# Two of eight hidden chunks of an MLP's second product as seven block products instead of eight

## The chip, the cores and the metric

One core of one Trainium2 chip runs the whole program. The metric is the device time of one execution in microseconds. The engines are named as the profile names them: PE is TensorE (PEld its weight loads), DVE is VectorE, ACT is ScalarE, SP is the engine that issues the loads.

## The reference

A decoder trunk of two layers on 512 tokens of width 1024, float32. Each layer has a mixer (not touched here), a layer norm, and an MLP with a residual and a second layer norm:

```python
def sqrelu_mlp(x, w1, w2):
    return jnp.square(jax.nn.relu(x @ w1)) @ w2
...
x = layer_norm(ALPHA * x + sqrelu_mlp(x, w_ff1[layer], w_ff2[layer]), ln2_g[layer], ln2_b[layer])
```

`w_ff1` is 1024x4096 and `w_ff2` 4096x1024, for each of the two layers.

## The kernel before

**Arithmetic.** Each float32 operand is split in two float32r parts, a rounded one ("hi", a cast on ScalarE) and the rest ("lo", a subtraction on VectorE). A product is then three matmuls: hi by hi, hi by lo, lo by hi.

**First product.** The hidden width is done in eight groups. Group g covers 256 columns of each half of `w_ff1`, and the activations are halved by rows and by columns, so a group is a 2x2 block matrix times a 2x2 block matrix. Group 0 is done with the eight plain block products. Groups 1 to 7 use the seven products of Strassen and Winograd, named P1, P2 and p3 to p7 (`PRODUCTS`). A product is 24 matmuls of 256 columns. The weight sums t1 to t4 are made on VectorE (line 374). The results are put together on VectorE (lines 485 to 498) from PSUM banks and two SBUF rows V and X. A bank may be shared: `RELEASED` says that p7 and p4 accumulate on one bank, "d", and P1 and P2 on another, "a". For block C22 the bank "d" is read when it holds p7 alone (line 485); for block C21 it is read when it holds p7 and p4 (line 493). V needs p6, X needs V and p5, and C22 needs X and p7.

**Activation.** `relu2` makes relu, square and the hi part of a hidden block on ScalarE (lines 428 to 430). The lo part (line 431, VectorE) is put on the list `late`, which is emitted at the next step by `flush`.

**Second product.** Chunk c of it uses the hidden blocks of group c. For each column half n and each token tile t it does twelve matmuls of 512 columns into one bank (`ff2_half`), and VectorE adds the bank to the residual XN (`add_half`, line 208). That is eight halves, 96 matmuls and eight additions for a chunk. Chunks 6 and 7 are done last, together with the layer norm.

**Order.** PE and VectorE keep the order of the program here; ScalarE's order is set by the framework's planner. The list `slots` is PE's order: group 1, chunk 1, group 2, chunk 2, groups 3 and 4, chunk 3, group 5, chunk 4, group 6, chunk 5, group 7, and the close. Inside a group the order (`LATER`) is P1, p5, p7, p6, p3, P2, p4. The list `wseq` is the order in which weight blocks are summed and split; `upto` issues loads up to six entries and splits up to six entries ahead of PE. At each slot the program emits, in this order, the weight work of `upto`, the lo parts of `flush`, the matmuls, and the VectorE work that reads their bank. Six PSUM banks rotate (`cycle`). Raw weight blocks (512 KB each) lie in three places of tag "raw" for `w_ff2` and in two of tag "cr" and two of tag "xk" for `w_ff1`. Eight pairs of split weights can be live.

Of the kernel before, what the change touches and what calls it, by code (L numbers as in the profile page):

```python
# [103 lines left out]
def trunk(ctx: ExitStack, tc: tile.TileContext, a: dict, out: bass.AP):  # L104
# [177 lines left out]
    ff_T = {}  # L282

    def ff(layer, hp, fp, xp, out_proj, prefetch):
# [66 lines left out]
        raws, got_w, kept2 = {}, {}, {}  # L351
        BLOCK = {"B11": (0, 0), "B12": (0, 1), "B22": (1, 1), "B21": (1, 0)}
        SUM = {"t1": ("B11", "B12"), "t3": ("B12", "B22"), "t2": ("t1", "B22"), "t4": ("t2", "B21")}

        def load1(g, n):

            for m in (n,) if g == 0 else {"B11": ("B11", "B12"), "B21": ("B21",), "t1": ("B22",)}.get(n, ()):
                if g == 0 and m != "B22":
                    raw = wp.tile([P, WG], F32, tag="raw", name="raw", bufs=3)
                elif g == 0 or m in ("B11", "B12"):  # L360
                    raw = xp.tile([P, WG], F32, tag="cr", name="cr", bufs=2)
                else:
                    if g not in kept2:
                        kept2[g] = xp.tile([P, 2, WG], F32, tag="xk", name="cr2")
                    raw = kept2[g][:, m == "B21"]
                raws[g, m] = raw
                nc.sync.dma_start(raw.rearrange("p (k c) -> p k c", k=HK_), w1v(*BLOCK[m], g))

# [17 lines left out]
        def terms1(g, n):  # L386
# [7 lines left out]
            else:  # L394
                hi, lo = pair(EARLY[n] if g == 0 else None)
                split(hi, lo, raw)
                his, los = ([z.rearrange("p (k c) -> p k c", k=HK_)[:, :, tb(j)] for j in range(2)] for z in (hi, lo))
            got_w[g, n] = his, los

        def load2(c, n, half):  # L400
            r = half * 2048 + c * GF
            raw = wp.tile([P, WG], F32, tag="raw", name="raw", bufs=3)
            nc.sync.dma_start(raw.rearrange("p (k c) -> p k c", k=2),
                              w2[r:r + GF, n * 512:(n + 1) * 512].rearrange("(k p) c -> p k c", p=P))
            raws["w2", c, n, half] = raw
# [29 lines left out]
        late = []  # L435

        def flush():
            while late:
                late.pop(0)()
# [23 lines left out]
        def product(g, n):  # L463
# [9 lines left out]
            V = LG[:, g % 2 * 512:(g % 2 + 1) * 512]  # L473
            X = LB[:, g % 2 * 512:(g % 2 + 1) * 512]
# [28 lines left out]

        def ff2_half(c, n, t):
# [9 lines left out]
        LATER = ("P1", "p5", "p7", "p6", "p3", "P2", "p4")  # L514
        slots, wseq = [], []

        def put_group(g):
            slots.extend((g, n) for n in LATER)
            wseq.extend((g, n) for n in ("B11", "t1", "t3", "t2", "B22", "B21", "t4"))

        def put_chunk(c):
            slots.extend(("w2", c, n, t) for n in range(2) for t in range(NT))
            wseq.extend(("w2", c, n, h) for n in range(2) for h in range(2))
# [3 lines left out]

        mid = NG // 2 - 1
# [824 lines left out]
```

## Time and profile before

| | us |
|---|---|
| median of three runs | 1167.61 (1167.41 to 1168.32) |
| the profiled execution | 1168.8 |
| its span, first to last instruction | 1167.1 |
| PE busy in the span | 1142.6 |
| VectorE busy in the span | 827.2 |

PE is busy for nearly the whole span, so the time is read stage by stage: what PE does there, and where it waits. A busy PE of the profile is modelled, so the pace of matmuls is taken from the length of a stretch and the number of its matmuls.

### The profile page before, as it was taken

The numbers are of one execution on the slowest core, as the hardware profiler recorded it, in microseconds if no ns is written. First come the engines' busy times: TensorE is split into PE (matmuls) and PEld (weight loads), VectorE is DVE, ScalarE is ACT, GpSimd is POOL, SyncE is SP. The second block draws the span as 40 slices with busy tenths as digits, with TensorE's granted clock in tenths as the row PEclk, the third lists the DMA queues.
The fourth block names the chain that finished last, engine by engine and source line by source line (L and its number), as shares of the span: only waits on it lengthen the run. The fifth ranks groups of instructions, "written<-read, shape, count | busy, mean of one in ns | idle before, by whom it ended". The sixth has DMA issues, their size and how long they took to land.

```text
span 1167.1 us, 17136 instructions
## 1 busy us (share of the span) xinstructions
PE 1142.6 (98%) x6888; PEld 996.6 (85%) x6888; DVE 827.2 (71%) x1562; ACT 516.1 (44%) x801; POOL 5.0 (0%) x13
## 2 busy tenths in 40 slices
PE   8999999999999999999999999999999999999997
PEld 8988788898889998998888888778997899889986
DVE  6745687786766767657758559898767577676655
ACT  5467462444343634533254433443544437345330
POOL 0000000000000000000000000000000000000000
PEclk9999999999999999999999999999999999999999
DMA  7413143133412342224235312212133224314121
GB/s 254 140 37 108 55 132 104 37 109 109 126 57 88 127 126 74 89 74 140 72 98 145 90 55 73 73 61 67 59 125 117 85 85 144 127 38 127 54 90 55
DMA packets 84207, 111.68 MB, mean 96 GB/s; under 512 B 6080, under 2 KB 53056, under 8 KB 84128
## 3 DMA queue, kind: packets, MB, share of 16 engines
q1 hardware_dynamic: 84128, 110.59, 30.1%
q8 instruction: 54, 0.88, 0.3%
q14 instruction: 25, 0.20, 0.1%
HBM read 108.47 MB, written 2.10 MB: 95 GB/s over the span
## 4 chain that ended last, share of the span: by engine, by line
PE 88%; DVE 7%; ACT 4%; DMA 0%; issue 0%; SPq 0%; DVEq 0%; ACTq 0%
PE f L451 23%; PE f L161 10%; PE f L159 10%; PE f L160 10%; PE vg L159 3%; PE vg L160 3%; PE vg L161 3%; PE op L159 2%; PE op L161 2%; PE op L160 2%; PE sc L836 1%; PE qk L159 1%; PE qk L160 1%; PE qk L161 1%; PE o L858 1%; PE pl L1117 1%
## 5 line engine op out<-in xcount | busy, mean ns | idle before, releaser
L161 PE MATMUL f<-whi,hl 128*128 128x512 f32 x448 | 178.0, 397 | 5.5 <-DVE hl L431 5.5
L159 PE MATMUL f<-whi,hh 128*128 128x512 f32 x448 | 177.9, 397 | 1.3 <-ACT hh L430 1.3
L164 ACT CAST whi<-cr 128x1024 fp32r<-128x1024 f32 x98 | 100.8, 1048 | 174.7 <-PE f L161 81.4
L160 PE MATMUL f<-wlo,hh 128*128 128x512 f32 x448 | 177.3, 396 | 0.0
L165 DVE TENSOR_TENSOR wlo<-cr,whi 128x1024 fp32r<-128x1024 f32 x98 | 119.2, 1220 | 23.0 <-ACT whi L164 23.0
L451 PE MATMUL f<-XH,wlo 128*128 128x256 f32 x448 | 125.9, 281 | 0.0
L451 PE MATMUL f<-XH,whi 128*128 128x256 f32 x448 | 125.8, 281 | 0.0
L451 PE MATMUL f<-XL,whi 128*128 128x256 f32 x448 | 125.8, 281 | 0.0
L161 PEld LDWEIGHTS f<-whi,hl 128*128 128x128 f32 x448 | 84.7, 189 | 27.8 <-DVE hl L431 8.1
L208 DVE SCALAR_TENSOR_TENSOR XN<-XN,f 128x512 f32<-128x512 f32 (+1 forms) x113 | 74.3, 678 | 43.9 <-PE f L161 43.1
L159 PEld LDWEIGHTS f<-whi,hh 128*128 128x128 f32 x448 | 84.7, 189 | 21.1 <-ACT hh L430 2.1
L160 PEld LDWEIGHTS f<-wlo,hh 128*128 128x128 f32 x448 | 84.8, 189 | 19.3
L451 PE MATMUL f<-sl,whi 128*128 128x256 f32 x336 | 94.5, 281 | 0.0
L451 PE MATMUL f<-sh,wlo 128*128 128x256 f32 x336 | 94.5, 281 | 0.0
L451 PE MATMUL f<-sh,whi 128*128 128x256 f32 x336 | 94.4, 281 | 0.0
L431 DVE TENSOR_TENSOR hl<-r,hh 128x512 fp32r<-128x512 f32 x64 | 44.1, 690 | 60.5 <-ACT hh L430 60.5
L451 PEld LDWEIGHTS f<-XL,whi 128*128 128x128 f32 x448 | 84.4, 188 | 0.5
L451 PEld LDWEIGHTS f<-XH,whi 128*128 128x128 f32 x448 | 84.4, 188 | 0.5
L451 PEld LDWEIGHTS f<-XH,wlo 128*128 128x128 f32 x448 | 84.4, 188 | 0.0
L164 ACT CAST whi<-raw 128x1024 fp32r<-128x1024 f32 x56 | 58.0, 1050 | 54.0 <-PE f L451 35.7
L137 ACT CAST whi<-raw 128x1024 fp32r<-128x1024 f32 (+3 forms) x61 | 60.2, 991 | 47.6 <-DMA raw<-in_w_in_odd 18.8
L138 DVE TENSOR_TENSOR wlo<-raw,whi 128x1024 fp32r<-128x1024 f32 (+3 forms) x61 | 69.7, 1148 | 14.6 <-ACT whi L137 14.3
(270 smaller groups left out, 2528.7 us busy)
## 6 DMA issues: line engine op xcount, KB each, us to landing
raw<-in_w_ff SPq DMA_DIRECT2D x70, 512.0 KB, 4.1
cr<-in_w_ff SPq DMA_DIRECT2D x58, 512.0 KB, 4.0
raw<-in_w_in_odd SPq DMA_DIRECT2D x24, 512.0 KB, 4.0
XN<-in_x SPq DMA_DIRECT2D x16, 256.0 KB, 3.0
raw<-in_w_in_even SPq DMA_DIRECT2D x8, 512.0 KB, 3.8
raw<-in_w_out_even SPq DMA_DIRECT2D x8, 512.0 KB, 3.6
raw<-in_w_out_odd SPq DMA_DIRECT2D x8, 512.0 KB, 3.5
LB<-in_ln_b SPq DMA_DIRECT2D x4, 512.0 KB, 3.8
```

Of the source, the lines that this page charges most:

```text
L137: nc.scalar.copy(hi[:, :n], raw[:, :n])
L138: nc.vector.tensor_tensor(lo[:, :n], raw[:, :n], hi[:, :n].bitcast(F32), ALU.subtract)
L159: nc.tensor.matmul(acc, lh, rh, start=first, stop=False)
L160: nc.tensor.matmul(acc, lh, rl, start=False, stop=False)
L161: nc.tensor.matmul(acc, ll, rh, start=False, stop=last)
L164: nc.scalar.copy(hi, src)
L165: nc.vector.tensor_tensor(lo, src, hi.bitcast(F32), ALU.subtract)
L208: nc.vector.scalar_tensor_tensor(x, x, ALPHA if first else 1.0, acc, ALU.mult, ALU.add)
L431: late.append(lambda: nc.vector.tensor_tensor(f(hl), r, f(hh).bitcast(F32), ALU.subtract))
L451: nc.tensor.matmul(d, l, r, start=first and j == k == i == 0, stop=j == 1 and k == HK_ - 1 and i == 2, skip_group_check=True)
L836: nc.tensor.matmul(sc[:, :N], qts[t][:B_QK, h, :], KT[:, h, :N], start=True, stop=True)
L858: nc.tensor.matmul(os[t][:, h, :], pT[:, j * P:(j + 1) * P], V[:, j, h, :], start=j == 0, stop=j == t)
```

## The change

Chunks 2 and 4 of each layer are now done as seven block products as well (`product2`), of twelve matmuls of 512 columns each, 84 for a chunk. For that the four hidden blocks of groups 2 and 4 are kept in float32 and four sums of them, s1 to s4, are made on VectorE and cast on ScalarE (`h_sum`); A21 alone needs no split. Four sums of the raw weight blocks of `w_ff2` are made on VectorE, and seven instead of four weight blocks are split. Each product leaves two banks. Those of P1 and p6 go to an SBUF row pair V2, those of the other five straight to XN; V2 is added to three blocks of XN after chunk 4. All raw weight blocks after chunk 0 take the same seven places, the one that is free first.

The order of PE changes too. Each chunk 1 to 5 stands right behind its own group, then come groups 6 and 7. Inside every group the order is now P1, p5, p7, p6, p4, P2, p3. Plain chunks take the token tiles in the order 2, 3, 0, 1. V and X are the same rows for every group.

```diff
+    SEVEN = (2, 4)
...
         def scratch(g):
 
-            return fp.tile([P, S], F32, name="r", **({"tag": "x", "bufs": 4} if g and next(turns) == "x" else {"tag": "q"}))
+            x = g in SEVEN or g and next(turns) == "x"
+            return fp.tile([P, S], F32, name="r", **({"tag": "x", "bufs": 4} if x else {"tag": "q"}))
...
         def relu2(g, i, j, src, into=None):
-            hh = hp.tile([P, 2, HALF_S], F32R, tag="hh", name="hh")
-            hl = hp.tile([P, 2, HALF_S], F32R, tag="hl", name="hl")
             r = into if into is not None else scratch(g)
-            f = lambda z: z.rearrange("p j t -> p (j t)")
             nc.scalar.activation(r, src, AF.Relu)
             nc.scalar.activation(r, r, AF.Square)
+            if g in SEVEN:
+                hs[g, i, j] = r
+                if (i, j) == (1, 0):
+                    late.append(lambda: h_sums1(g))
+                    return
+            hh, hl = hq[g][i, j] = term_tiles()
             nc.scalar.copy(f(hh), r)
-            late.append(lambda: nc.vector.tensor_tensor(f(hl), r, f(hh).bitcast(F32), ALU.subtract))
-            hq[g][i, j] = hh, hl
+            late.append(lambda: h_lo(hh, hl, r))
+            if g in SEVEN and i == 0:
+                late.append(lambda: (h_sums3 if j else h_sums2)(g))
...
+        def h_sum(g, n, into, x, y, op=ALU.subtract):
+            nc.vector.tensor_tensor(into, x, y, op)
+            hh, hl = hq[g][n] = term_tiles()
+            nc.scalar.copy(f(hh), into)
+            late.append(lambda: h_lo(hh, hl, into))
...
-            V = LG[:, g % 2 * 512:(g % 2 + 1) * 512]
-            X = LB[:, g % 2 * 512:(g % 2 + 1) * 512]
+            V, X = LG[:, :512], LB[:, :512]
...
+        V2 = [z[:, 512:] for z in (LG, LB)]
+        TWO = {"P1": "a", "P2": "a", "p5": "d", "p3": "d", "p7": "f", "p4": "f", "p6": "b"}
+        ADDS = {"P2": (0, 0, ALU.add), "p5": (2, 1, ALU.subtract), "p7": (2, 1, ALU.subtract),
+                "p3": (0, 1, ALU.subtract), "p4": (2, 0, ALU.add)}
+
+        def product2(c, n):
+            g = "w", c
+            op, w = PRODUCTS[n]
+            hh, hl = hq[c][{"A11": (0, 0), "A12": (0, 1), "A22": (1, 1)}.get(op, op)]
+            wh, wl = got_w.pop((g, w))
+            first = (g, TWO[n]) not in banks
+            if first:
+                banks[g, TWO[n]] = [bank("f2") for _ in range(2)]
+            for i, acc in enumerate(banks[g, TWO[n]]):
+                for k in range(2):
+                    for m, (l, r) in enumerate(((hh, wh), (hh, wl), (hl, wh))):
+                        nc.tensor.matmul(acc, l[:, k, tb(i)], r[:, k], start=first and k == m == 0, stop=k == 1 and m == 2,
+                                         skip_group_check=True)
+            for i, acc in enumerate(banks[g, TWO[n]]):
+                if n == "P1" and c == min(SEVEN):
+                    nc.scalar.mul(V2[i], acc, -1.0)
+                elif n in ("P1", "p6"):
+                    nc.vector.tensor_tensor(V2[i], V2[i], acc, ALU.subtract if n == "P1" else ALU.add)
+                else:
+                    t, half, sign = ADDS[n]
+                    x = XN[:, t + i, half * 512:(half + 1) * 512]
+                    nc.vector.tensor_tensor(x, x, acc, sign)
...
-        LATER = ("P1", "p5", "p7", "p6", "p3", "P2", "p4")
+        LATER = ("P1", "p5", "p7", "p6", "p4", "P2", "p3")
+        AGAIN = ("P1", "p5", "P2", "p7", "p6", "p3", "p4")
...
-            wseq.extend((g, n) for n in ("B11", "t1", "t3", "t2", "B22", "B21", "t4"))
+            wseq.extend((g, n) for n in ("B11", "t1", "t3", "t2", "t4", "B21", "B22"))
...
+            if c in SEVEN:
+                slots.extend((("w", c), n) for n in AGAIN)
+                wseq.extend((("w", c), n) for n in ("B11", "B21", "t1", "t3", "t2", "B22", "t4"))
...
-        mid = NG // 2 - 1
         for c in range(1, NG - 2):
-            for g in (c,) if c < mid else (c, c + 1) if c == mid else (c + 1,):
-                put_group(g)
+            put_group(c)
             put_chunk(c)
+        put_group(NG - 2)
         put_group(NG - 1)
```

## Rows read from the trace of the kernel before

**Rows 1.** The page: part 1, busy us (share) xinstructions; part 4, the chain.

```profile
PE 1142.6 (98%) x6888; PEld 996.6 (85%) x6888; DVE 827.2 (71%) x1562; ACT 516.1 (44%) x801; POOL 5.0 (0%) x13
...
PE 88%; DVE 7%; ACT 4%; DMA 0%; issue 0%; SPq 0%; DVEq 0%; ACTq 0%
```

**Rows 2.** Stretches: groups 1, 2, 6, chunks 1, 2, 4; columns in first line.

```profile
core 0: us, PE busy (x) PEld busy (x) DVE busy (x) ACT busy (x) POOL busy (x), PEclk, DMA share, GB/s
269.85:290.10 20.25, 20.05 (x169) 19.84 (x167) 12.60 (x14) 10.61 (x16) 0.00 (x0) 1.00 0.40 126
290.10:314.00 23.90, 22.68 (x97) 18.11 (x97) 19.64 (x23) 8.85 (x10) 0.00 (x0) 1.00 0.29 91
314.00:334.32 20.32, 20.05 (x170) 19.85 (x168) 9.61 (x12) 10.77 (x15) 0.00 (x0) 1.00 0.40 129
334.32:359.76 25.44, 24.23 (x96) 19.24 (x97) 18.59 (x22) 7.95 (x9) 0.00 (x0) 0.93 0.21 63
...
441.75:464.06 22.31, 22.31 (x99) 18.09 (x97) 15.47 (x19) 8.26 (x10) 0.00 (x0) 1.00 0.19 61
464.06:483.95 19.89, 19.89 (x170) 19.89 (x169) 12.83 (x15) 10.47 (x15) 0.00 (x0) 1.00 0.47 145
...
858.85:879.10 20.25, 20.05 (x170) 19.84 (x168) 12.61 (x14) 10.62 (x16) 0.00 (x0) 1.00 0.41 126
879.10:902.99 23.89, 22.68 (x96) 18.11 (x97) 19.63 (x23) 8.84 (x10) 0.00 (x0) 1.00 0.28 91
902.99:923.67 20.68, 20.06 (x170) 19.85 (x168) 9.61 (x12) 10.78 (x15) 0.00 (x0) 1.00 0.40 128
923.67:947.56 23.89, 22.68 (x97) 18.11 (x98) 18.49 (x22) 7.95 (x9) 0.00 (x0) 1.00 0.21 67
```

**Rows 3.** The timeline where group 1 gives over to chunk 1, layer 0.

```profile
290.10 0.50 PE L159 MATMUL f<-whi,hh 128*128 128x512 f32 x1 [0.20 <-ACT hh L430]
290.18 1.22 DVE L165 TENSOR_TENSOR wlo<-raw,whi 128x1024 fp32r<-128x1024 f32 x1
...
291.31 0.68 DVE L431 TENSOR_TENSOR hl<-r,hh 128x512 fp32r<-128x512 f32 x1
...
292.05 0.50 PE L161 MATMUL f<-whi,hl 128*128 128x512 f32 x1 [1.22 <-DVE hl L431]
```

**Rows 4.** The timeline in the close of layer 0.

```profile
529.16 0.40 PE L160 MATMUL f<-wlo,hh 128*128 128x512 f32 x1
...
529.88 0.50 PE L161 MATMUL f<-whi,hl 128*128 128x512 f32 x1 [0.32 <-DVE hl L431]
```

**Rows 5.** The timeline of group 5 around the end of its p6.

```profile
433.11 0.28 PE L451 MATMUL f<-sh,wlo 128*128 128x256 f32 x1
...
433.43 0.69 DVE L497 TENSOR_TENSOR LG<-f,LG 128x512 f32<-128x512 f32 x1 [3.51 <-PE f L451]
...
434.16 0.69 DVE L498 TENSOR_TENSOR LB<-LG,f 128x512 f32<-128x512 f32 x1
...
434.88 0.69 DVE L485 TENSOR_TENSOR r<-LB,f 128x512 f32<-128x512 f32 x1
...
435.60 0.63 ACT L428 ACTIVATE r<-r 128x512 f32<-128x512 f32 x1 [1.20 <-DVE r L485]
```

**Rows 6.** The timeline of VectorE alone in chunk 4, layer 0.

```profile
443.32 1.22 DVE L165 TENSOR_TENSOR wlo<-cr,whi 128x1024 fp32r<-128x1024 f32 x1
444.46 0.68 DVE L431 TENSOR_TENSOR hl<-r,hh 128x512 fp32r<-128x512 f32 x1
445.06 0.69 DVE L493 TENSOR_TENSOR f<-f,LG 128x512 f32<-128x512 f32 x1
447.73 0.69 DVE L431 TENSOR_TENSOR hl<-r,hh 128x512 fp32r<-128x512 f32 x1 [1.98 <-ACT hh L430]
```

**Rows 7.** The stretch behind the wait at the start of chunk 2, columns as Rows 2.

```profile
337.00:339.60 2.60, 2.60 (x7) 2.01 (x7) 0.69 (x1) 1.70 (x3) 0.00 (x0) 0.50 0.00 0
```

**Rows 8.** The page, part 6: DMA issues, KB each, median us to landing.

```profile
cr<-in_w_ff SPq DMA_DIRECT2D x58, 512.0 KB, 4.0
```

More of the change, by code (lines that the diff above doesn't have):

```diff
@@ L355, in load1 @@
         def load1(g, n):
[L357 to L361, printed above, removed]
-                else:
-                    if g not in kept2:
-                        kept2[g] = xp.tile([P, 2, WG], F32, tag="xk", name="cr2")
-                    raw = kept2[g][:, m == "B21"]
+            for m in loads_at(g, n):
+                i, j = BLOCK[m]
+                if g == 0:
+                    raw = xp.tile([P, WG], F32, tag="cr", name="cr", bufs=2) if m == "B22" else ring_raw()
+                else:
+                    raw = place_of(max(place[g, u] for u in USES[m]))
@@ L369, in sum1, with place_of @@
+        places = []
+        def place_of(until):
+            if not places:
+                two = xp.tile([P, 2, WG], F32, tag="xk", name="cr2")
+                tiles = [ring_raw() for _ in range(3)]
+                tiles += [xp.tile([P, WG], F32, tag="cr", name="cr", bufs=2) for _ in range(2)] + [two[:, 0], two[:, 1]]
+                places.extend([0, t] for t in tiles)
+            p = min(places, key=lambda p: p[0])
+            p[0] = until
+            return p[1]
         def sum1(g, n):
@@ L400, in load2 @@
         def load2(c, n, half):
[L401 to L405, printed above, removed]
+            raw = raws["w2", c, n, half] = ring_raw() if c == 0 else place_of(place["w2", c, n, half])
+            load_w2(raw, half * 2048 + c * GF, n)
         def terms2(c, n, half):
@@ L437, in flush, with h_sums3 @@
+        def h_sums3(g):
+            a12, a22 = hs[g, 0, 1], hs[g, 1, 1]
+            h_sum(g, "s4", a12, a22, a12)
+        late, hs = [], {}
         def flush():
-            while late:
-                late.pop(0)()
+            now, late[:] = late[:], []
+            for step in now:
+                step()
         banks, state = {}, {}
@@ L502, in product, with add_V2 @@
             step("C21", {"V", "C22", "p4"}, c21)
+        V2 = [z[:, 512:] for z in (LG, LB)]
[20 more added lines that the diff above has]
+                    nc.vector.tensor_tensor(V2[i], V2[i], acc, ALU.subtract if n == "P1" else ALU.add)
+                else:
+                    t, half, sign = ADDS[n]
+                    x = XN[:, t + i, half * 512:(half + 1) * 512]
+                    nc.vector.tensor_tensor(x, x, acc, sign)
+        def add_V2():
+            for t, half, sign in ((0, 1, ALU.add), (2, 1, ALU.add), (2, 0, ALU.subtract)):
+                for i in range(2):
+                    x = XN[:, t + i, half * 512:(half + 1) * 512]
+                    nc.vector.tensor_tensor(x, x, V2[i], sign)
         def ff2_half(c, n, t):
@@ L535, in ff @@
         for i, w in enumerate(wseq):
-            if w[0] != "w2" and w[1] == "B11" and i and wseq[i - 1][0] == "w2":
+            if w[1] == "B11" and i and not isinstance(w[0], tuple) and not isinstance(wseq[i - 1][0], int):
                 wseq[i - 1:i + 1] = wseq[i - 1:i + 1][::-1]
@@ L541, in ff, with load_some, upto @@
         LOADS, TERMS = 6, 6
-        def upto(n, loads=None):
-            while at["load"] < min(len(wseq), n + (LOADS if loads is None else loads)):
+        def load_some(to):
+            while at["load"] < min(len(wseq), to):
                 w = wseq[at["load"]]
+                n = 1 if w[0] == "w2" else len(loads_at(*w))
+                if n and w[0] != 0 and w[:2] != ("w2", 0) and places and sorted(places, key=lambda p: p[0])[n - 1][0] >= at["terms"]:
+                    break
                 at["load"] += 1
                 (load2(*w[1:]) if w[0] == "w2" else load1(*w))
+        def upto(n, loads=None):
+            to = n + (LOADS if loads is None else loads)
+            load_some(to)
             while at["terms"] < min(len(wseq), n):
@@ L580, in ff @@
                 else:
-                    upto(min(need + 1 + TERMS, need + 1 + 2 * (s[3] + 1)))
+                    upto(min(need + 1 + TERMS, need + 1 + 2 * (s[4] + 1)))
                 flush()
                 ff2_half(s[1], s[2], s[3])
+                continue
+            if isinstance(s[0], tuple):
+                upto(place[s[0], PRODUCTS[s[1]][1]] + TERMS)
+                flush()
+                product2(s[0][1], s[1])
+                if s == (("w", max(SEVEN)), AGAIN[-1]):
+                    add_V2()
                 continue
```

43 lines of the change are left out of this document (35 added, 8 removed).

## The prediction

> **What bounds the kernel now.** I read the page's busy shares and its chain first: PE is busy for 98% of the span and makes up 88% of the chain [rows 1]. So a matmul saved is time saved, as long as nothing makes PE wait. Then I read the stretches of the MLP [rows 2]. An undisturbed group takes 19.89 us for seven products, 2.84 us each. An undisturbed chunk takes 22.31 us for 96 matmuls, 0.2324 us each. VectorE is busy for 15.47 + 12.83 = 28.3 us of the 42.2 us of such a pair. Where a chunk follows its own group (chunks 1 and 2) the stretches are longer. The timeline shows why [rows 3]: the third matmul needs the lo part of a hidden block, VectorE did a weight split ahead of it, and the chunk's first two steps took 292.05 - 290.10 = 1.95 us instead of 0.46, a wait of about 1.5 us. Last I looked for what each product waits for, above all the chain behind p6 [rows 5]: V, X and C22 are three VectorE operations, each of which needs the one before. p6's last matmul starts at 433.11 and C22's result is handed on at 435.60. Today p3 and P2 run on other banks for 5.7 us meanwhile, and nobody waits.
>
> **The change, term by term.** The sum is made against the profiled execution, 1168.8 us; it lies 1.2 us over the median of the runs.
>
> *Fewer matmuls.* 96 - 84 = 12 in each of four chunks: 48 x 0.2324 = **11.2 us less** [rows 2]. This is the whole gain that PE can have of the seven products.
>
> *Waits at the border of group and chunk.* In the new order, plain chunks start with token tiles 2 and 3, whose blocks are done two products earlier, and chunks 2 and 4 start differently (below). The old excess goes. In layer 0 groups 1 and 2 and chunks 1 and 2 took 20.25 + 23.90 + 20.32 + 25.44 = 89.91 us against 2 x 42.20 undisturbed: 5.5 us. In layer 1 it is 88.71, 4.3 us [rows 2]. The close waits 0.72 - 0.23 = 0.5 us for a lo part in each layer [rows 4]; with P2 two products earlier from the end than p4 was in the old order, that goes too. Together **10.8 us less**.
>
> *p4 right behind p6.* This is the step that I think decides. p4 accumulates on bank "d", on top of p7. C22 must read that bank while it holds p7 alone, and C22 needs X, which needs V, which needs p6. So p4's first matmul cannot start until the third VectorE operation behind p6 is done. Without the wait the next product starts at 433.23; C22 is done and handed on at 435.60 [rows 5]. The cover that hid this, p3 and P2, now stands behind p4. Each of seven groups in two layers pays 435.60 - 433.23 = 2.4 us: **14 x 2.37 = 33.2 us more**. Below, it would cost less only if VectorE's chain were shorter, and its three operations are unchanged. Above, a weight split that VectorE is still in (a step of 1.14 us, [rows 6]) would make it 3.5 us; in the old kernel VectorE had been idle 3.5 us before V [rows 5], so I take the lower end.
>
> On this the Trainium skill, page "Perfetto Trace Analysis", section "Matmuls", says that independent groups of matmuls should rotate through different PSUM banks, so that reading one overlaps the next group's matmuls. The rows agree for the order of before, in which the read of "d" overlapped p3. The rule speaks against p4 there, and the page gives no price.
>
> *VectorE's added work in chunks 2 and 4.* Back to back, one operation on 1024 columns takes 1.14 us of VectorE and one on 512 columns 0.60 us [rows 6]. Chunk 2 gains three splits and four weight sums (7 x 1.14), four hidden sums and three lo parts (7 x 0.60), and twelve additions in place of eight (4 x 0.60): 14.6 us. Chunk 4 has two more subtractions for P1 and six additions of V2: 19.4 us. With the 28.3 us of a pair that makes 43 and 48 us, against 39.4 us of PE (42.2 - 2.8). The pairs on either side have some 14 us to spare, but only what may be done early moves there: `upto` looks six entries ahead, and a read of a bank can't be early at all. So some of it must show as waits of PE. I follow VectorE's program order through group 2 and chunk 2, with zero at the start of the group:
> - C22 is done at 13.7. Then come a sum and a split, the lo part of (1,1), C21 (not before p4 ends, 16.8), a sum and a split, s1, a sum and a split, the lo part of s1, and the lo part of (0,0): done at about 23.8. PE has finished p3 at 22.3 and the two matmuls that need no lo part at 22.7: **1.1 us**.
> - After that come s3, s2, C12, two splits, three lo parts and s4, to 30.3, then the entries of slot p5: two sums, two splits, a lo part, p5's additions and P2's. P2's first bank is free at about 37.3. p6 takes new banks, and six banks rotate, so it takes P1's and P2's: PE is there at 34.8. **2.5 us**.
> - The next group's P1 takes the bank of p3's first addition: **1.0 us**.
>
> The same for chunk 4 gives 0.4 + 2.0 + 1.0, and its six additions of V2 delay V in group 5 by 1.8 us. So I take 5 us for a chunk, **20 us more** for four. Below, it is zero if the spare time of the neighbours takes it all. Above, each of the three hand-overs to ScalarE and back in this chain (cast, then lo part) can cost what one costs VectorE now at its worst, 1.98 us [rows 6], and a fourth one for V2's read by ScalarE: 5 + 4 x 2 = 13 us for a chunk, 52 us.
>
> *The clock.* After four such waits at the borders (chunks 1 and 2 of both layers), the granted clock fell once to half (1.2 of 2.4 GHz), in the stretch behind chunk 2's start in layer 0 [rows 7]. That chunk took 25.44 us, its twin in layer 1 with the same wait 23.89: 1.55 us [rows 2]. The new waits are 14 of 2.4 us and some four of 2 us or more, all longer than those. None of them losing the clock costs nothing, all 18 cost 28 us. Between one in four and all I take eight: **12 us more**.
>
> The page "TensorE: Matmul & The Clock Gate" of the Trainium skill, section "A second HAM failure mode: psum-queue depth-cycling", tells of a kernel in which short idles between groups of matmuls made the clock swing between its two levels. One wait of four in this trace agrees. [...]
>
> *At no cost.* Loads: the number and bytes are the same; 512 KB land in 4.0 us [rows 8], and the new shared places are filled at least three entries ahead of use, over 5 us of PE time. If a place came free late, PE would wait up to those 4 us, once or twice. ScalarE: six more casts for a chunk, on an engine that is busy 8.3 + 10.5 of 42.2 us [rows 2].
>
> **Sum.** 1168.8 - 11.2 - 10.8 + 33.2 = 1180.0 for what is sure; + 20 + 12 = **1212 us**.
>
> **Rivals.**
> - *Faster: the cover holds.* If p4 were not held by C22's read, because the chain behind p6 is done in time or the bank is not the one I think, the price of 33.2 us and most of the clock's would go, and the time would be 1146.8 us with VectorE's surplus hidden, or 1167 with it. It decides at 22 us of waits: under that the change gains. For it: VectorE idles before V now. Against it: idling before V doesn't help, since V waits for p6 itself [rows 5]. 6 in 100.
> - *The clock falls after every long wait.* 1180 + 20 + 28 = 1228 us. For it: the new waits are all longer than the one that lost the clock. Against it: three like waits kept it. 20 in 100.
> - *VectorE's queue is worse than I tallied.* Hand-overs to ScalarE add up: 1180 + 52 + 12 = 1244 us. For it: VectorE does wait for ScalarE's casts [rows 6]. Against it: ScalarE is mostly free. 17 in 100.
> - *VectorE's surplus is hidden and the clock mostly holds.* 1180 to 1195 us. For it: 14 us to spare on either side. 15 in 100.
> - *The forecast,* 1195 to 1225 us: 40 in 100. The last 2 are for no difference.
>
> **The range.** From 1180 (both unknown costs at zero) to 1244 (VectorE at its upper end, the clock in the middle; a PE that runs at half clock gives VectorE time, so I don't add both upper ends). The chances: slower 0.92, the same 0.02, faster 0.06, where faster and slower mean by more than 0.2%, about what a measurement of this kernel can tell from no change.
>
> **What would show it.** Right, if in every group PE stands still about 2.4 us before its fifth product and what ended it is line C22's subtraction on VectorE, if VectorE is busy nine tenths or more through chunks 2 and 4, if PE waits there for a lo part and for additions to XN, and if half-clock stretches follow some of the waits. Wrong, if PE runs from p6 into p4 without a gap; then the rest is a gain. A chunk 2 or 4 whose matmuls alone take more than 19.6 us at full clock would break the first term.

## The result and the profile after

| | before | after |
|---|---|---|
| median of four runs of each, same chip | 1167.96 us | **1235.91 us** (1233.43 to 1240.76) |
| the profiled execution | 1168.8 | 1233.43 |
| its span | 1167.1 | 1231.5 |
| mean granted clock over the span | 0.997 | 0.983 |

The ratio is **1.058**, with a 95% interval of 1.0561 to 1.0603: the changed kernel is slower by 68 us. The time lies in the predicted range (1180 to 1244) and on the predicted side, but 24 us above the predicted 1212 and above the forecast's own band of 1195 to 1225. The four executions after lie 7 us apart; the two longer ones ran at a lower mean clock (0.978 and 0.974).

The page of the changed kernel, its first part (busy us, share of the span, instructions) and the row of TensorE's granted clock in 40 slices:

```profile
PE 1151.8 (94%) x6840; PEld 1000.0 (81%) x6840; DVE 896.9 (73%) x1650; ACT 539.6 (44%) x829; POOL 4.5 (0%) x13
PEclk9999999999999998999999999999999999989999
```

PE has its 48 matmuls fewer (6840 for 6888 in [rows 1]), yet its share fell from 98 to 94%: it waits. VectorE has 70 us more work. What PE waited for in the MLP, the six largest sums (who waited <- for whom: us in all, times, longest):

```profile
PE f L510 <- DVE r L543: 37.8, 14, 5.1
PE f L579 <- DVE XN L589: 8.3, 4, 2.4
PE f L510 <- DVE XN L589: 5.0, 4, 1.9
PE f L161 <- DVE hl L456: 3.0, 2, 1.5
PE f L579 <- DVE hl L456: 2.8, 4, 1.2
PE f L159 <- ACT hh L468: 2.7, 2, 1.4
```

In this kernel L510 is a matmul of a group, L543 the subtraction of C22, L579 a matmul of `product2`, L589 its addition to XN, L456 the lo part of a hidden block and L468 a hi part; L159 to L161 are the matmuls of the plain chunks and the close. The first row is the wait that the prediction called decisive: 14 times, seven groups in two layers. The timeline of group 1 (start, length, engine and line, out<-in; in brackets the idle time before it and what ended it) is [rows 5] over again, with p4 where p3 was:

```profile
282.31 0.28 PE L510 MATMUL f<-sh,wlo 128*128 128x256 f32 x1
282.62 0.69 DVE L555 TENSOR_TENSOR LG<-f,LG 128x512 f32<-128x512 f32 x1 [2.79 <-PE f L510]
283.35 0.69 DVE L556 TENSOR_TENSOR LB<-LG,f 128x512 f32<-128x512 f32 x1
284.07 0.69 DVE L543 TENSOR_TENSOR r<-LB,f 128x512 f32<-128x512 f32 x1
284.90 0.36 PE L510 MATMUL f<-XH,whi 128*128 128x256 f32 x1 [2.32 <-DVE r L543]
```

p6 ends, V, X and C22 follow on VectorE, and p4's first matmul starts at 284.90, when C22's read of bank "d" is over. The stretches of group 1, chunk 1, chunk 2 and group 5 of layer 0 (columns as in [rows 2]), and the 6.5 us in group 5 in which the clock was at half:

```profile
271.05:293.51 22.46, 20.14 (x170) 19.96 (x168) 15.77 (x18) 14.40 (x19) 0.00 (x0) 1.00 0.43 141
293.51:315.81 22.30, 22.30 (x99) 18.08 (x97) 17.84 (x20) 8.06 (x9) 0.00 (x0) 1.00 0.32 100
338.33:362.50 24.17, 20.35 (x87) 15.57 (x86) 24.03 (x30) 11.11 (x15) 0.00 (x0) 1.00 0.31 97
...
457.70:484.88 27.18, 22.06 (x168) 21.89 (x169) 22.13 (x27) 14.81 (x20) 0.00 (x0) 0.87 0.41 129
472.00:478.50 6.50, 4.05 (x19) 4.08 (x20) 4.07 (x6) 1.88 (x3) 0.00 (x0) 0.50 0.75 241
```

Group 1 takes 22.46 us against 19.89 undisturbed. Chunk 1 takes 22.30 where it took 23.90 [rows 2]: the border gain came. Chunk 2 has twelve matmuls fewer and takes 24.17, longer than a plain chunk, with VectorE busy for 24.03 of it.

The largest single loss is group 5's wait for p4. VectorE's timeline there (same columns; the first line is one of six V2 additions):

```profile
464.02 0.69 DVE L595 TENSOR_TENSOR XN<-XN,LG 128x512 f32<-128x512 f32 x1
467.63 2.36 DVE L165 TENSOR_TENSOR wlo<-raw,whi 128x1024 fp32r<-128x1024 f32 x2
469.90 2.36 DVE L165 TENSOR_TENSOR wlo<-cr,whi 128x1024 fp32r<-128x1024 f32 x2
472.17 0.69 DVE L555 TENSOR_TENSOR LG<-f,LG 128x512 f32<-128x512 f32 x1
```

Four weight splits (4.5 us) stand between the V2 additions and V. PE is done with p6 at 469.33, while VectorE is still in them; V starts at 472.17, 2.8 us after PE stopped, where in group 1 it starts at once. The close of layer 0 shows a wait that nobody had forecast (same columns):

```profile
553.43 0.28 PE L510 MATMUL f<-sh,wlo 128*128 128x256 f32 x1
553.75 1.05 ACT L164 CAST ws<-cr 128x1024 fp32r<-128x1024 f32 x1 [0.93 <-PE f L510]
554.83 1.23 DVE L165 TENSOR_TENSOR ws<-cr,ws 128x1024 fp32r<-128x1024 f32 x1 [6.06 <-ACT ws L164]
557.71 0.69 DVE L456 TENSOR_TENSOR hl<-r,hh 128x512 fp32r<-128x512 f32 x1
558.45 0.50 PE L161 MATMUL f<-whi,hl 128*128 128x512 f32 x1 [1.48 <-DVE hl L456]
```

The tiles "ws" of the last weights lie where the operands of p3 lie. p3 is now the last product of the last group, so ScalarE's cast starts only at 553.75, when p3 ends; VectorE idles 6.06 us, then does the splits, and the lo part that PE needs stands behind them. C12, the block that p3 completes, comes behind them too, and PE waits once more, 1.35 us, for its hi part.

### The profile page after: what moved, and what is told of

The parts are those of the page before. It is cut to its first block, busy times and chain, and to the rows that moved or that the text cites. A ratio compares the mean times of both kernels' runs of the same rounds, so it can differ in the third digit from the quotient of the medians.

```text
span 1231.5 us, 17183 instructions
## 1 busy us (share of the span) xinstructions
PE 1151.8 (94%) x6840; PEld 1000.0 (81%) x6840; DVE 896.9 (73%) x1650; ACT 539.6 (44%) x829; POOL 4.5 (0%) x13
## 5 line engine op out<-in xcount | busy, mean ns | idle before, releaser
L510 PE MATMUL f<-XH,whi 128*128 128x256 f32 x448 | 132.3, 295 | 39.0 <-DVE r L543 37.8
L164 ACT CAST whi<-raw 128x1024 fp32r<-128x1024 f32 x78 | 81.1, 1049 | 130.5 <-DVE raw L400 97.0
L510 PE MATMUL f<-XL,whi 128*128 128x256 f32 x448 | 130.7, 292 | 0.0
L510 PE MATMUL f<-XH,wlo 128*128 128x256 f32 x448 | 130.6, 292 | 0.0
L161 PE MATMUL f<-whi,hl 128*128 128x512 f32 x320 | 127.7, 399 | 3.0 <-DVE hl L456 3.0
L159 PE MATMUL f<-whi,hh 128*128 128x512 f32 x320 | 127.2, 398 | 2.7 <-ACT hh L468 2.7
L160 PE MATMUL f<-wlo,hh 128*128 128x512 f32 x320 | 127.1, 397 | 0.0
L164 ACT CAST whi<-cr 128x1024 fp32r<-128x1024 f32 x88 | 91.1, 1046 | 81.7 <-DVE cr L400 44.4
L510 PEld LDWEIGHTS f<-XH,whi 128*128 128x128 f32 x448 | 89.7, 200 | 42.8 <-issue 32.9
L165 DVE TENSOR_TENSOR wlo<-cr,whi 128x1024 fp32r<-128x1024 f32 x88 | 107.1, 1221 | 8.2 <-ACT whi L164 8.0
L165 DVE TENSOR_TENSOR wlo<-raw,whi 128x1024 fp32r<-128x1024 f32 x78 | 94.4, 1222 | 23.0 <-ACT whi L164 23.0
L510 PE MATMUL f<-sh,whi 128*128 128x256 f32 x336 | 94.7, 282 | 3.8 <-DVE XN L589 3.7
L510 PE MATMUL f<-sl,whi 128*128 128x256 f32 x336 | 94.7, 282 | 0.0
L510 PE MATMUL f<-sh,wlo 128*128 128x256 f32 x336 | 94.6, 282 | 0.0
L510 PEld LDWEIGHTS f<-XL,whi 128*128 128x128 f32 x448 | 89.6, 200 | 0.5
L510 PEld LDWEIGHTS f<-XH,wlo 128*128 128x128 f32 x448 | 89.5, 200 | 0.0
L456 DVE TENSOR_TENSOR hl<-r,hh 128x512 fp32r<-128x512 f32 x76 | 51.7, 690 | 48.9 <-ACT hh L468 48.2
L208 DVE SCALAR_TENSOR_TENSOR XN<-XN,f 128x512 f32<-128x512 f32 (+1 forms) x81 | 53.8, 677 | 35.8 <-PE f L161 35.5
L161 PEld LDWEIGHTS f<-whi,hl 128*128 128x128 f32 x320 | 60.7, 190 | 18.9 <-DVE hl L456 4.9
L159 PEld LDWEIGHTS f<-whi,hh 128*128 128x128 f32 x320 | 60.6, 190 | 16.9 <-ACT hh L468 3.6
```

Source lines behind the costliest of these rows:

```text
L159: nc.tensor.matmul(acc, lh, rh, start=first, stop=False)
L160: nc.tensor.matmul(acc, lh, rl, start=False, stop=False)
L161: nc.tensor.matmul(acc, ll, rh, start=False, stop=last)
L164: nc.scalar.copy(hi, src)
L165: nc.vector.tensor_tensor(lo, src, hi.bitcast(F32), ALU.subtract)
L208: nc.vector.scalar_tensor_tensor(x, x, ALPHA if first else 1.0, acc, ALU.mult, ALU.add)
```

## The experiments

All ratios are against the kernel before, run beside it on the same chip, and the short diffs are against the changed kernel unless they say otherwise. A "wait" is PE's, as in the second fence above; line numbers are those of each kernel. The expectations count the half-clock stretches of the changed kernel's MLP as ten; there are eight, two of them of double length.

### The chunks alone, and the order alone

**All chunks plain, the new order kept** (label e2_plain_chunks).

```diff
-    SEVEN = (2, 4)
+    SEVEN = ()
```

> The changed kernel with all chunks as eight halves (96 matmuls) and nothing else undone: its order of slots and products and its seven shared places stay. Theory: the waits before p4 stay, 12 to 14 of 2.4 to 2.6 us, the two of 5 us shrink to 2.5 us as no V2 is added ahead of them; 1168 - 10 (waits at the borders) + 35 (p4) + 5 (the close) + about 8 (clock) = 1200 to 1212 us. Rival (the seven products themselves cost the time): within 10 us of the kernel before.

Measured: 1212.83 us, ratio 1.0376 (1.0360 to 1.0391). Its waits:

```profile
PE f L510 <- DVE r L543: 32.5, 14, 2.4
PE f L161 <- DVE hl L456: 3.0, 2, 1.5
```

The order alone costs 44 of the 68 us. Its 14 waits before p4 are all alike, so what the two of 5 us have above the others belongs to the seven products (by the timeline above, to V2's additions and the splits behind them); the close's waits stay, so they belong to the order. The time is a little over the expected band.

**P2 between p6 and p4 again** (e1_cover).

```diff
-        LATER = ("P1", "p5", "p7", "p6", "p4", "P2", "p3")
+        LATER = ("P1", "p5", "p7", "p6", "P2", "p4", "p3")
...
-                    late.append(lambda: h_sums1(g))
+                    late.append(lambda: (h_sums1(g), h_sums2(g)))
```

(and the weights in that order.)

> In every group P2 stands between p6 and p4, so 24 matmuls (2.8 us) run on another bank while C22 is put together; all else is as in the changed kernel. Theory (p4's wait on the bank that C22 reads is the largest part of the loss): the 14 waits before p4, 40.0 us of the changed kernel's trace, fall below 3 us, the half-clock stretches of the MLP fall from ten to five or fewer (some 7 us), and the time is 1183 to 1195 us. Rival (VectorE's added work is the bound, p4 only the place where it shows): VectorE is as busy as before, the waits move to other products, and the time stays above 1215 us.

Measured: 1217.47 us, ratio 1.0407 (1.0380 to 1.0434): 22 us above the theory's band and in the rival's range. Its waits:

```profile
PE f L159 <- ACT hh L467: 23.2, 8, 4.7
PE f L509 <- DVE r L542: 3.1, 2, 2.0
```

The waits before p4 are gone but for two, and others have come at the start of the chunks; the MLP has nine half-clock stretches, three of double length. The timeline at the border of group 1 and chunk 1:

```profile
290.12 0.69 DVE L550 TENSOR_TENSOR f<-f,LG 128x512 f32<-128x512 f32 x1
290.84 0.60 ACT L459 ACTIVATE r<-f 128x512 f32<-128x512 f32 x1 [2.58 <-DVE f L550]
292.13 0.62 ACT L467 CAST hh<-r 128x512 fp32r<-128x512 f32 x1
292.80 0.50 PE L159 MATMUL f<-whi,hh 128*128 128x512 f32 x1 [1.56 <-ACT hh L467]
```

With p4 second to last, C21 (L550) is done at 290.84, and relu, square and cast take until 292.8; the chunk starts with that very block. So p4's early place was worth something: it serves the chunk that now follows its own group at once. Theory and rival had both looked only at the group: the rival has the time, but VectorE's added work is not the cause of these waits, since chunks 1 and 3, which are plain, have them too, and the next run has them without any seven-product chunk.

**The same with plain chunks** (e6_plain_cover): `SEVEN = ()`, P2 before p4 in groups 1 to 5, the old order in groups 6 and 7, and the halves of token tiles 2 and 3 begin with C22, which is done first.

```diff
+            ks = (2, 3, 0, 1) if c and i else range(4)
```

> All chunks as eight halves; P2 between p6 and p4 in groups 1 to 5, the order of before (p4 last) in groups 6 and 7, and the halves of tiles 2 and 3 begin with block (1,1), which is ready first. The order of groups and chunks and the seven places are those of the changed kernel. Theory (the loss is made of p4's wait, the border, the close and the clock, and the seven places cost nothing): no wait of over 1 us in the MLP and no half-clock stretch in it: 1168 - 10 (the old borders) = 1156 to 1161 us. Rival (the shared places or the new order of chunks cost something of their own): 1168 us or more.

Measured: 1178.21 us, ratio 1.0080 (1.0063 to 1.0097): 17 us above the theory's band, and again in the rival's range:

```profile
PE f L159 <- ACT hh L467: 11.2, 10, 2.1
```

Ten waits, one for each chunk 1 to 5, for the hi part of the block that p4 makes. The close waits only 0.7 us, in layer 0, since p3 is not last there. The rival's cause, a cost of the shared places, is ruled out by e8_plain_own_bank below, which has the same places. This run is 35 us better than the new order alone, but neither of these two orders with the shared bank serves both the bank and the chunk.

### What p4 waits for, taken away

**A bank of its own for p4** (e3_own_bank). C21 was (p7 + p4) - V; here V is first replaced by p7 - V on VectorE, and p4 is added later. It costs one more VectorE operation for a group.

```diff
-        RELEASED = {"P1": "a", "P2": "a", "p3": "c", "p4": "d", "p5": "e", "p6": "b", "p7": "d"}
+        RELEASED = {"P1": "a", "P2": "a", "p3": "c", "p4": "f", "p5": "e", "p6": "b", "p7": "d"}
...
+                nc.vector.tensor_tensor(V, bk("d"), V, ALU.subtract)
...
-                nc.vector.tensor_tensor(bk("d"), bk("d"), V, ALU.subtract)
-                relu2(g, 1, 0, bk("d"))
+                nc.vector.tensor_tensor(bk("f"), bk("f"), V, ALU.add)
+                relu2(g, 1, 0, bk("f"))
```

> The changed kernel with its order kept, but p4 accumulates on a bank of its own: V becomes bank d minus V once C22 has read d, and C21 is p4's bank plus V. One more VectorE operation of 0.6 us in a group. Theory (p4 waits because it writes the bank that C22 reads, not because it comes early): no wait before p4 in any of the 14 groups (40.0 us go), the borders stay as they are (under 0.7 us), the waits in chunks 2 and 4 stay near 22 us and those of the close at 3 us a layer, half-clock stretches fall to five or so; 1186 to 1198 us. Rival (the chain behind p6 is needed at once anyway, so the wait moves to P2, p3 or the chunk): above 1210 us.

Measured: 1203.87 us, ratio 1.0296 (1.0276 to 1.0316), 6 us over the theory's band:

```profile
PE f L159 <- ACT hh L468: 9.4, 5, 4.4
PE f L580 <- ACT hh L468: 7.8, 4, 2.0
```

All 14 waits before p4 are gone: it was the shared bank. Of their 37.8 us the time gives back 32. The rest turns into waits that they had hidden: 2 us for a hidden block's hi part at the start of chunks 2 and 4, and up to 4.4 us before chunk 5. The half-clock stretches did not fall to five: behind the new waits there are nine in the MLP, four of them of double length.

**The same bank, all chunks plain, the close in the old order** (e8_plain_own_bank): `SEVEN = ()`, the edit above, and groups 6 and 7 in the old order.

```diff
-            slots.extend((g, n) for n in LATER)
+            end = g >= NG - 2
+            slots.extend((g, n) for n in (("P1", "p5", "p7", "p6", "p3", "P2", "p4") if end else LATER))
```

> All chunks as eight halves, the changed kernel's order with p4 on a bank of its own in groups 1 to 5, and in groups 6 and 7 p4 last as before. Theory: as with the order changed instead of the bank, 1156 to 1161 us; the close waits 0.5 us a layer as before. Rival (the close's 3 us a layer come from the order of the groups, not from p3 standing last): 1162 us or more.

Measured: **1162.05 us**, ratio **0.9942** (0.9926 to 0.9957): faster than both kernels, 1 us over the expected band. That is just at the rival's bound, but the rival's cause fails: the close's 3 us a layer are gone. Its longest wait in the MLP, the one in the close of layer 0:

```profile
PE f L161 <- DVE hl L456: 0.7, 1, 0.7
```

And its stretches of group 4 and chunk 4 (columns as in [rows 2]):

```profile
396.65:416.54 19.89, 19.89 (x169) 19.88 (x168) 13.42 (x16) 10.46 (x15) 0.00 (x0) 1.00 0.43 131
416.54:439.07 22.53, 22.53 (x99) 18.01 (x97) 15.46 (x19) 8.27 (x10) 0.00 (x0) 1.00 0.25 76
```

The group runs at the undisturbed 19.89 us with p4 right behind p6, and there is no half-clock stretch in the MLP. The new order's gain at the borders is real, once p4 does not share a bank.

On this the Trainium skill, page "Perfetto Trace Analysis", section "Matmuls", says that independent groups of matmuls should rotate through different PSUM banks, so that the read of one overlaps the matmuls of the next. The runs agree: the same order takes 1235.91 us with p4 on p7's bank and 1203.87 us with a bank of its own (e3_own_bank).

**The wait filled, not removed** (e5_filled_wait): 20 matmuls of 256 columns on a bank that nobody reads, between p6 and p4.

```diff
+            if n == "p4":
+                spare = bank("spare", "tp")
+                for k in range(20):
+                    nc.tensor.matmul(spare[:, :HALF_S], XH[:, k % 4, :P], XH[:, k % 4, :HALF_S], start=k == 0, stop=k == 19,
+                                     skip_group_check=True)
```

> The changed kernel with 20 matmuls of 256 columns (2.36 us) into a bank that nobody reads, between p6 and p4 of every group: PE works where it waited, and p4 starts no later than 0.1 us after its old time. Theory (half-clock stretches come from PE's waits, and cost about 1.6 us each): six or more of the ten half-clock stretches of the MLP go, and the time falls by 6 to 15 us to 1221 to 1230 us. Rival (the clock falls for another reason, or PE's waits before p4 are not what counts): the stretches stay and the time is 1233 us or more.

Measured: 1225.30 us, ratio 1.0481 (1.0466 to 1.0497): the time as expected. PE's timeline in group 1:

```profile
281.01 0.28 PE L510 MATMUL f<-sh,wlo 128*128 128x256 f32 x1
281.12 2.55 PE L532 MATMUL spare<-XH 128*128 128x256 f32 x20
283.61 0.36 PE L510 MATMUL f<-XH,whi 128*128 128x256 f32 x1
```

p4 starts no earlier behind its p6 (283.61 - 281.01 = 2.60 us, as 284.90 - 282.31 = 2.59 before), yet the time is 10.6 us shorter. The mean clock rose from 0.983 to 0.990. Five half-clock stretches of the MLP are left, one of double length, of eight: four of the expectation's ten went, not six. The two profiled executions are 8.2 us apart. Half clock loses 4.8 us less in the MLP there and 1.2 us less ahead of it, and the rest is shorter waits in groups 3 and 5 of layer 1. So the idle of these waits does cost the clock something beside itself, some 5 us by these two traces; more than that is not shown.

### The seven products, once the order is out of the way

**Seven products, p4 on a bank of its own, the close in the old order** (e9_seven_own_bank): the kernel above with `SEVEN = (2, 4)`.

> As the one before, with chunks 2 and 4 as seven products: the change without p4's wait and without the close's. Theory (PE saves 11.2 us and waits 20 us for VectorE in and behind these chunks, with three to five half-clock stretches): 1158 - 11 + 20 + 6 = 1168 to 1178 us, so the seven products lose against eight halves. Rival (with p4's wait gone VectorE has time, and the waits in the chunks shrink under 8 us): 1150 to 1157 us, faster than the eight halves.

Measured: 1192.36 us, ratio 1.0206 (1.0188 to 1.0223), 14 us over the expected band: the waits in and behind these chunks are 31 us, not 20, and half clock loses 11 us, not 6. Its two largest waits are those of e3_own_bank, at the start of chunks 2 and 4 and before chunk 5:

```profile
PE f L580 <- ACT hh L468: 7.8, 4, 2.0
PE f L159 <- ACT hh L468: 7.1, 2, 4.4
```

Two comparisons come out of this run. Against e3_own_bank, which differs in the order of groups 6 and 7 alone, it is 11.5 us faster: that is the price of p3 as the last product, some 7 us of waits in the two closes where 1 us is left, and a half-clock stretch of double length in each layer behind them. Against the plain kernel above, the seven products alone cost **30 us**. In the spans (1190.0 and 1159.2) it adds up: -11.2 for the matmuls, +30.9 of start-to-start losses in and behind the seven-product chunks, and +10.7 at half clock make 30.4 of the 30.8 found. Even in the best order found the saved matmuls lose.

Four more runs asked which part of the seven products it is.

**No sums of `w_ff2`** (e4_no_weight_sums, against the changed kernel). The four sums of raw weights of chunks 2 and 4 are left out.

```diff
-                nc.vector.tensor_tensor(raws[g, n], raws[g, x], raws[g, y], ALU.add)
+                if not isinstance(g, tuple):
+                    nc.vector.tensor_tensor(raws[g, n], raws[g, x], raws[g, y], ALU.add)
```

> Left out: the four sums of raw weight blocks of chunks 2 and 4, 16 VectorE operations of 1.14 us, so the seven products use unsummed blocks; all matmuls, splits and additions stay. Theory (PE's 21.6 us of waits inside and behind these two chunks are VectorE's backlog): they fall to 10 us or less, the two waits of 5 us before p4 in group 5 fall to 2.5 us, and the time falls by 10 to 20 us to 1216 to 1226 us. Rival (they are the shape of the chain, bank read after product, whatever VectorE has queued): the waits stay within 4 us of 21.6 and the time above 1228 us.

Measured, one run: 1229.44 us, 6.5 less than the changed kernel's median. Its waits:

```profile
PE f L511 <- DVE r L544: 36.2, 14, 5.1
PE f L580 <- DVE XN L590: 3.8, 4, 1.3
```

The waits in the chunks fall from 21.8 to about 15.7 us, the largest of them, for a bank of XN, from 8.3 to 3.8. So 16 of VectorE's operations explain some 6 us of these waits, between theory and rival; the time is the rival's. The wait of 5.1 us in group 5 stays in layer 0, and in layer 1 it falls from 4.9 to 3.4. The clock took some of it back: twelve half-clock stretches in the MLP, one of double length, lose some 5 us more than the changed kernel's eight. With one execution, against four that lie 7 us apart, the time itself says little.

**Those sums on GpSimd** (e10_pool_sums, against e9_seven_own_bank).

```diff
-                nc.vector.tensor_tensor(raws[g, n], raws[g, x], raws[g, y], ALU.add)
+                (nc.gpsimd if isinstance(g, tuple) else nc.vector).tensor_tensor(raws[g, n], raws[g, x], raws[g, y], ALU.add)
```

> The seven-product kernel with p4 on its own bank (1192 us), but the four sums of raw weight blocks of chunks 2 and 4 are made on GpSimd, which is idle in the MLP, instead of VectorE (16 operations of 1.14 us). Theory (PE waits in and behind these chunks for VectorE's queue): they fall from 32 to some 20 us, one or two half-clock stretches go, 1174 to 1186 us, still above the 1162 us of the eight halves. Rival (GpSimd's sums are so slow, or disturb VectorE so much, that weights come late): 1192 us or more, with PE waiting for a split of a weight block.

Measured: 1191.05 us, ratio 1.0199 (1.0184 to 1.0214): no gain, 5 us above the theory's band and without the rival's wait for a weight. Its waits:

```profile
PE f L580 <- ACT hh L468: 13.0, 4, 3.7
PE f L580 <- DVE XN L590: 2.2, 3, 1.3
```

One of its groups of GpSimd's instructions (xcount | busy us, mean ns of one | idle before them and what ended most of it):

```profile
L400 POOL TENSOR_TENSOR cr<-cr,raw 128x1024 f32<-128x1024 f32 x8 | 20.9, 2607 | 22.4 <-DVE wlo L165 22.1
```

The bank waits fall from 6.2 us to 2.2 and the waits for ScalarE's hi parts rise from 7.8 to 13.0. A sum takes 2.6 us on GpSimd and 1.22 on VectorE, and ScalarE's cast of it stands ahead of a hidden block's cast in ScalarE's queue. So it is at the start of chunk 2 in layer 0, where PE waits until 334.17:

```profile
332.03 1.04 ACT L164 CAST whi<-cr 128x1024 fp32r<-128x1024 f32 x1 [1.52 <-POOL cr L400]
333.50 0.61 ACT L468 CAST hh<-r 128x512 fp32r<-128x512 f32 x1
```

**No sums and no lo parts of those weights at all** (e11_no_weight_work, against e9_seven_own_bank). The hi part is used in place of the lo part, so that the number of matmuls stays.

```diff
-                nc.vector.tensor_tensor(raws[g, n], raws[g, x], raws[g, y], ALU.add)
+                if not isinstance(g, tuple):
+                    nc.vector.tensor_tensor(raws[g, n], raws[g, x], raws[g, y], ALU.add)
...
+                if isinstance(g, tuple):
+                    hi = wp.tile([P, WG], F32R, tag="whi", name="whi")
+                    nc.scalar.copy(hi, raw)
+                    got_w[g, n] = [hi.rearrange("p (k c) -> p k c", k=2)] * 2
+                    return
```

> Left out, in chunks 2 and 4: the four weight sums and all seven lo parts of the weights (the hi part is multiplied twice); the 84 matmuls stay. VectorE has 11 operations of 1.14 us less in each chunk than the seven-product kernel with p4 on its own bank, and four less than for eight halves. Theory (VectorE's backlog): PE's 32 us of waits there fall under 10 us, the half-clock stretches go, and the time is 1153 to 1163 us, so that the saved matmuls show. Rival (the length of the chain of the hidden sums, from C21 over s1 and s3 to their lo parts and back to PE, whatever else is queued): 16 us or more of waits stay and the time is 1170 us or more.

Measured: 1179.24 us, ratio 1.0098 (1.0074 to 1.0123): the rival's time, and 18.5 us of waits, as the rival has it.

```profile
PE f L583 <- ACT hh L471: 8.7, 4, 2.2
PE f L159 <- ACT hh L471: 7.4, 3, 4.4
```

With 11 VectorE operations of 1024 columns less in each such chunk, the waits inside the chunks are nearly gone and 13 us with them, but the kernel still loses 17 us to plain chunks. What stays is at the borders, and not where the rival had put it. PE waits 2.2 us at the start of each of the four chunks, for the hi part of C11: ScalarE makes its relu and square together with those of C21, then casts a weight and s1, and casts C11 last. Around the start of chunk 5 it waits 4.6 us in one layer, 2.8 and 2.0 us in the other, where V is late behind the six additions of V2 and four splits. Behind these waits there are six half-clock stretches, one of double length, which lose some 10 us. This split is read from the trace; no run takes away one of the two alone.

**Lo parts ahead of weight work, V2 on GpSimd** (e12_seven_relief, against e9_seven_own_bank).

```diff
-                    nc.vector.tensor_tensor(x, x, V2[i], sign)
+                    nc.gpsimd.tensor_tensor(x, x, V2[i], sign)
...
             if isinstance(s[0], tuple):
-                upto(place[s[0], PRODUCTS[s[1]][1]] + TERMS)
                 flush()
+                upto(place[s[0], PRODUCTS[s[1]][1]] + TERMS)
...
+            if s[0] in SEVEN:
+                flush()
```

> The seven-product kernel with p4 on its own bank (1192 us), with two things moved and nothing left out: in groups 2 and 4 and their chunks the lo parts and hidden sums are emitted ahead of the weight work of the slot, and the six additions of V2 are made by GpSimd. Theory (what is left are two queues: the hidden chain behind weight work on VectorE at the start of chunks 2 and 4, and V2's additions ahead of V in group 5): the four waits of 2.1 us at the start of these chunks and the two of 2.8 and 4.6 us at the start of chunk 5 fall under 1 us, 10 us or more of PE's waits and one or two half-clock stretches go, 1172 to 1182 us. Rival (the chain through ScalarE sets the start, and VectorE is short of time in any order, so that weights or bank reads come late instead): 1187 us or more. Neither expects it under the 1162 us of the eight halves.

Measured: 1211.29 us, ratio 1.0358 (1.0340 to 1.0375): 19 us worse, the rival's time. Its waits:

```profile
PE f L580 <- ACT hh L468: 17.3, 6, 3.6
PE f L580 <- DVE XN L590: 9.8, 4, 4.7
```

A line of VectorE's timeline in chunk 2:

```profile
333.63 0.69 DVE L475 TENSOR_TENSOR r<-r 128x512 f32<-128x512 f32 x1 [1.67 <-ACT r L461]
```

VectorE keeps the order of the program, so an operation put ahead of its time makes it idle, here 1.67 us for ScalarE's square, and everything behind it is later. Around chunk 5 the waits fell, from 4.5 to 2.8 us in layer 0 and from 4.4 to 3.2 us in layer 1, so the loss lies in chunks 2 and 4; two things were moved at once, and no run parts them. I know of no order of this work that hides it; that none exists is not shown.

## Why the prediction was right, and where its sizes were off

The losses below are start-to-start times in the trace of the changed kernel, so they are a little larger than the idle times in its list of waits.

| term | predicted | measured |
|---|---|---|
| fewer matmuls | -11.2 | -11.2 |
| borders | -9.8 | -9.8 |
| close | -1.0 | **+5.3** |
| p4 right behind p6, with V2's delay in group 5 | +36.8 | +40.0 |
| VectorE in chunks 2 and 4 | +16.4 | +21.8 |
| clock | +12 | +13.4 |

(The prediction has borders and close together as 10.8, and V2's delay, 1.8 us in each layer, in its 20 us for the chunks. The one half-clock stretch of before, 1.4 us, is in its borders.) The terms make 43.2 and 59.5 us. The spans differ by 64.4; 1.2 of the rest is a half-clock stretch at the start of the program, ahead of the MLP. Of the last 3.7 us, 2.8 are second matmuls behind a wait, which start 0.07 to 0.11 us late by the pace, some 30 times; 0.9 are not accounted for.

- **Fewer matmuls: right.** Chunk 2 without its waits takes 24.17 - 4.31 = 19.86 us, 84 matmuls at 0.2324 are 19.5. That is over the 19.6 us that the prediction set as a sign against this term, but what is over 19.5 us are the second matmuls behind its three waits, each 0.10 to 0.11 us late; the others keep the pace.
- **Borders: right.** Chunks 1, 3 and 5 take 22.30 to 22.32 us, without a wait.
- **Close: wrong in sign.** The step that failed is "with P2 two products earlier from the end than p4 was in the old order, that goes too". It followed the hidden block and not the weights. p3 became the last product, and its operands hold the places that the last weights need. The close waits 1.64 and 1.51 us in each layer, where it waited 0.5 [rows 4]. With p4 on a bank of its own, e9_seven_own_bank puts the whole price, with the clock, at 11.5 us.
- **p4 behind p6: right in mechanism, low in size.** Twelve of the 14 waits lose 2.39 to 2.55 us against the predicted 2.37. The other two, in group 5, lose 5.28 and 5.02. The step "delay V in group 5 by 1.8 us" took too little: it is 2.7, with the four splits between the V2 additions and V. e3_own_bank shows that the shared bank is the cause, and e2_plain_chunks that the two long ones belong to the seven products; that it is V2 and the splits is read from the timeline.
- **VectorE in chunks 2 and 4: mostly the right places, a third more in sum.** Chunk 2 waited 1.31 us for the first lo part (predicted 1.1), 2.57 for p6's bank (2.5), and 2.03 in one layer and 0.79 in the other in the next group (1.0). Chunk 4: 0.93 for a hi part at P2 and 1.91 (0.4 and 2.0), then 0.79 and 2.03. VectorE was busy for 24.03 of the 24.17 us of chunk 2, as the prediction's signs had it. What was not in the tally: 0.66 us at the start of chunk 4, for C11's hi part, 0.43 at P2 of chunk 2, and that in one layer the next group waits at p7 for 2.03 and not at P1. The bank wait of chunk 2, with VectorE in additions to XN:

```profile
352.08 2.47 DVE L589 TENSOR_TENSOR XN<-XN,f 128x512 f32<-128x512 f32 x4
354.01 0.51 PE L579 MATMUL f<-whi,hh 128*128 128x512 f32 x1 [2.41 <-DVE XN L589]
```

- **The clock: right by luck of the mean.** Eight half-clock stretches in the MLP lose 13.4 us; I had taken eight of 18 waits at 1.55 us. Six lose 1.4 to 1.5 us each; the two of double length, in group 5, lose 1.9 and 2.7, since PE stands still for part of them. Two come where the prediction had no wait at all, in the close. The page "TensorE: Matmul & The Clock Gate" of the Trainium skill, section "A second HAM failure mode: psum-queue depth-cycling", tells of short idles that made the clock swing between its two levels. This trace agrees in part: the clock fell behind four of the twelve waits of 2.2 to 2.4 us before p4, and the other eight kept it.

So the 24 us between 1212 and the median are the close (6.3), the chunks (5.4), p4 behind p6 (3.2), the clock (1.4), 1.2 of half clock at the start, the last 3.7, and 2.5 by which the profiled execution lies under the median of its four.

Of the rivals, "the cover holds" fell with the first fence of waits. "The clock falls after every long wait" (1228) and "VectorE's queue is worse than I tallied" (1244) lie 8 us below and above what was measured, and neither is its cause: the clock lost 13.4 us and not 28, and VectorE's work cost some 27 us with V2's delay and not 52. The close was in no rival. What the prediction didn't see is a hidden benefit: the waits before p4 gave ScalarE and VectorE time that the next chunk's start needed, so taking them away brings only part of their length (e3_own_bank).

## What to carry to other kernels

When a product is moved, list every resource that it holds, its bank and its operands' places, and who reads or refills each next. A bank that is read halfway through its accumulation makes the next product on it wait for the whole chain of that read; a bank of its own for one VectorE operation more (0.6 us, hidden) was worth more than any order tried. On a PE that is 98% busy, matmuls saved by sums elsewhere must be weighed against the time that the engines which make the sums have in that very stage: here 11 us of matmuls cost 30 us net even in the best order found. With 11 VectorE operations less in each such chunk (e11_no_weight_work) 13 of the 30 us go. The rest stays with the chain of VectorE and ScalarE to the first block of the next chunk, and with the clock behind those waits.

## What the hardware showed that was not expected

- Useless matmuls in waits of 2.3 us made the program 10.6 us faster (8.2 between the profiled executions), without starting the next useful matmul earlier: the granted clock fell to half five times in the MLP and not eight.
- Behind a wait of PE the second matmul started 0.07 to 0.11 us late by the pace, some 30 times in the changed kernel (284.90 to 285.10 in group 1, where the pace is 0.118).
- GpSimd took 2.4 to 2.7 us for a sum of 1024 columns that takes VectorE 1.22 (e10_pool_sums), and 1.65 to 1.95 us for 512 columns, for which VectorE takes 0.69 (e12_seven_relief); all are means.
- Three VectorE operations on 512 columns, each of which needs the one before, start 0.72 us apart (282.62, 283.35, 284.07 in group 1), where two independent ones start 0.60 us apart [rows 6].
